# Split passes in the outer stages of a long convolution, and its spectrum loaded once

## The chip, the cores and the metric

The kernel runs on one core of a Trainium2 chip. The metric is the device time of one execution in microseconds (us). It took 3428.81 us in the median of 3 runs (3427.15 to 3435.29).

The core's engines work side by side, each through its own instructions in a fixed order: TensorE (PE, with PEld for its weight loads), VectorE (DVE), ScalarE (ACT), GpSimd (POOL) and SyncE (SP), whose queue issues nearly all DMA transfers here. An instruction that waits holds up all that stand behind it on its engine.

## The reference

One layer of an encoder, sequence 2048, width 1024, fp32. A projection feeds two groups of heads: a Hyena group (512 channels) and an mLSTM group (512 channels). Their outputs are normalised, projected, added; cross-attention and a squared-ReLU MLP follow. What matters here is the Hyena group:

```python
def _hyena(hy, spec, skip):
    L = hy.shape[1]
    u = hy.astype(jnp.float32)
    z, g1, g2 = u[..., :D_HYENA], u[..., D_HYENA:2 * D_HYENA], u[..., 2 * D_HYENA:]
    for o, gate in enumerate((g1, g2)):
        conv = jnp.fft.irfft(jnp.fft.rfft(z, n=2 * L, axis=1) * spec[:, o], n=2 * L, axis=1)[:, :L]
        z = gate * (conv + z * skip[o].astype(jnp.float32))
    return z
```

So there are two rounds, each a real FFT of length 4096, a product with the spectrum of a filter, an inverse FFT, and a gate. The second round's result is normalised in groups of 64 channels.

## The kernel before, in words

`program` (L1615) puts the phases in order, and `weave` (L1597) mixes two of them as Python generators: each yields a cost after a piece of work, and the one that is behind in its share goes on. `filters` (L158) makes the spectra of both rounds and writes them to DRAM (`hd`), mixed with the first projection passes. `hyena` (L628) is mixed with the rest of the input projection (`sweep` L502, `natural` L595). Then come `mlstm` (L761) mixed with the last projection pieces and `memproj`, and `attention` mixed with the rest of mLSTM, and the MLP. The program is not run in the written order: `schedule_with_timeline_sim` (L1584) lets a scheduler reorder each engine's instructions before the build, so the diff alone does not give the order on an engine.

`hyena` writes each FFT as two small DFTs with data in DRAM between them. The sequence is laid out as 128 partitions x 16 columns `j`, each of 512 channels. One round `o` has three stages:

- Stage 1 (L700 to L713), 8 steps of two columns. `load1` brings `z` (512 KB); each column is multiplied by the two parts of `f1` (L710, fp32, 128x512), ScalarE and VectorE in turn copy the results out of PSUM (`copy`, L137), and two stores write them to `zs`.
- Stage 2 (L715 to L732), 16 steps of two frequency blocks. `load2` (L655) brings the step's matrices `dm` and `em`, the data `t` (512 KB), and the spectrum: `hr` gets the real part and `hi` the imaginary part, each 64 rows, loaded twice so that both partition halves hold them (L664 to L666, four transfers of 256 KB). For each of two blocks: a matmul by `dm` (L724), two ScalarE copies that exchange the halves (L726, L727), a VectorE product with `hr` (L728), a GpSimd product with `hi` (L729), a VectorE sum (L730), and, one block later (`late`), the matmul back by `em` (L692) with its ScalarE evacuation (L693). When both are out, a store to `zg` (L695). The loads of step i+1 are asked for at the start of step i.
- Stage 3 (L734 to L759), 8 steps of two columns. `load3` brings two parts of `zg` and the gate; for each column two accumulated matmuls by the parts of `e2` (L743) and a VectorE product with the gate (L744). In the first round the result goes to `z1`, the second round's input. In the second it is squared on GpSimd (L751), summed and normalised on VectorE (L753 to L756, with `rsqrt` L144), multiplied by a gain on GpSimd (L758) and stored.

All these tiles come from two rings: tag `a` (128 x 2 x 512, 10 buffers) and tag `b` (128 x 512, 5 buffers); PSUM gives the convolution four banks (`hy`, L124) and the projection four others (`mm`, L121). mLSTM's first tiles take the memory that the convolution leaves, so it begins when `hyena` is through.

The projection does not use fp32 matmuls. It splits each operand into a high part, rounded to fp32r by a ScalarE cast, and a low part, the rest, by a VectorE subtraction (`split`, L299), and adds three passes:

```python
    def mm3(self, ps, lh, ll, rh, rl, start, stop):
        mm = self.nc.tensor.matmul
        mm(ps, lh, rh, start=start, stop=False)
        mm(ps, lh, rl, start=False, stop=False)
        mm(ps, ll, rh, start=False, stop=stop)
```

The functions that the diff touches, and what calls them:

Of the kernel before, what the change touches and what calls it, by code (L numbers as in the profile page):

```python
# [9 lines left out]
F32 = mybir.dt.float32  # L10
F32R = mybir.dt.float32r
I32 = mybir.dt.int32
AF = mybir.ActivationFunctionType
ALU = mybir.AluOpType
# [6 lines left out]
CH = 512  # L21
# [76 lines left out]
class Prog:  # L98
# [22 lines left out]
    def mm(self):  # L121
        return self.ps.tile([128, 512], F32, tag="mm", name="mm", bufs=4)
# [170 lines left out]
    def mm3(self, ps, lh, ll, rh, rl, start, stop):  # L293
        mm = self.nc.tensor.matmul
        mm(ps, lh, rh, start=start, stop=False)  # L295
        mm(ps, lh, rl, start=False, stop=False)  # L296
        mm(ps, ll, rh, start=False, stop=stop)  # L297

    def split(self, hi, lo, src):  # L299
        self.nc.scalar.copy(hi, src)  # L300
        self.nc.vector.tensor_tensor(lo, src, hi.bitcast(F32), ALU.subtract)  # L301
# [326 lines left out]
    def hyena(self, es):  # L628
        nc, tc, a = self.nc, self.tc, self.a
        hy = self.dram("hy", (3, L, CH)).rearrange("s (q j) c -> s q j c", j=16)  # L630
        hd = self.dram("hd", (2, 32, 128, CH))
        yh = self.dram("yh", (L, CH)).rearrange("(q j) c -> q j c", j=16)
        z1 = self.dram("z1", (128, 16, CH))
        sds = [self.dram(f"zs{o}", (2, 128, 16, CH)) for o in range(2)]
        gds = [self.dram(f"zg{o}", (2, 128, 16, CH)) for o in range(2)]
        sb = es.enter_context(tc.tile_pool(name="h_sb", bufs=1, side="right"))

        def ta():
            return sb.tile([128, 2, CH], F32, tag="a", name="a", bufs=10)

        def tb():
            return sb.tile([128, CH], F32, tag="b", name="b", bufs=5)

        f1 = sb.tile([128, 2, 128], F32, name="f1")
        e2 = sb.tile([128, 2, 128], F32, name="e2")
        nc.sync.dma_start(out=f1, in_=a["c_f1"])
        nc.sync.dma_start(out=e2, in_=a["c_e2"])
        ghy = self.bcast(sb, a["hy_norm_g"], CH, "ghy")
        def load1(o, j2):
            z = ta()  # L650
            js = slice(2 * j2, 2 * j2 + 2)
            nc.sync.dma_start(out=z, in_=hy[0, :, js] if o == 0 else z1[:, js])
            return z

        def load2(o, i):  # L655
            p, k = divmod(2 * i, 16)
            dm = sb.tile([128, 2, 128], F32, tag="dm", name="dm", bufs=2)
            em = sb.tile([128, 2, 128], F32, tag="em", name="em", bufs=2)
            nc.sync.dma_start(out=dm, in_=a["c_dm"][:, 2 * i:2 * i + 2])
            nc.sync.dma_start(out=em, in_=a["c_em"][:, 2 * i:2 * i + 2])  # L660
            t, hr, hi = ta(), ta(), ta()
            nc.sync.dma_start(out=t, in_=sds[o][p, 8 * k:8 * k + 16].rearrange("(k r) j c -> (r j) k c", k=2))
            src = hd[o, 2 * i:2 * i + 2].rearrange("k (r l) c -> r l k c", r=2)
            for h in range(2):  # L664
                nc.sync.dma_start(out=hr[64 * h:64 * h + 64], in_=src[0])
                nc.sync.dma_start(out=hi[64 * h:64 * h + 64], in_=src[1])  # L666
            if i == 0:
                nc.sync.dma_start(out=hr[64:65, 0], in_=hd[o, 0, 64:65])
                nc.vector.memset(hi[0:1, 0], 0.0)
                nc.vector.memset(hi[64:65, 0], 0.0)  # L670
            return dm, em, t, hr, hi

        def load3(o, j2):
            js = slice(2 * j2, 2 * j2 + 2)
            r = [ta() for p in range(2)]
            for p in range(2):
                nc.sync.dma_start(out=r[p], in_=gds[o][p, :, js])
            gate = ta()
            nc.sync.dma_start(out=gate, in_=hy[1 + o, :, js])
            return r, gate  # L680

        held = []

        def late(f):
            if held:
                held.pop()()
            if f is not None:
                held.append(f)

        def back(m, em, y, gs, dst):  # L690
            pg = self.hy()
            nc.tensor.matmul(pg, em[:, m], y, start=True, stop=True)  # L692
            nc.scalar.copy(gs[:, m], pg)  # L693
            if m == 1:
                nc.sync.dma_start(out=dst.rearrange("(k r) j c -> (r j) k c", k=2), in_=gs)  # L695

        for o in range(2):
            sd, gd = sds[o], gds[o]
            q = [load1(o, 0), load1(o, 1)]
            for j2 in range(8):  # L700
                yield 3.5
                js = slice(2 * j2, 2 * j2 + 2)
                z = q.pop(0)
                if j2 < 6:
                    q.append(load1(o, j2 + 2))
                st = [ta() for p in range(2)]
                for jj in range(2):
                    for p in range(2):
                        pp = self.hy()
                        nc.tensor.matmul(pp, f1[:, p], z[:, jj], start=True, stop=True)  # L710
                        self.copy(st[p][:, jj], pp)
                for p in range(2):
                    nc.sync.dma_start(out=sd[p, :, js], in_=st[p])  # L713
            nxt = load2(o, 0)
            for i in range(16):  # L715
                yield 3.5
                p, k = divmod(2 * i, 16)
                dm, em, t, hr, hi = nxt
                if i < 15:
                    nxt = load2(o, i + 1)  # L720
                gs = ta()
                for m in range(2):
                    pp = self.hy()
                    nc.tensor.matmul(pp, dm[:, m], t[:, m], start=True, stop=True)  # L724
                    xt, y = tb(), tb()
                    nc.scalar.activation(xt[0:64], pp[64:128], AF.Copy, scale=-1.0)  # L726
                    nc.scalar.copy(xt[64:128], pp[0:64])  # L727
                    nc.vector.tensor_tensor(y, pp, hr[:, m], ALU.mult)  # L728
                    nc.gpsimd.tensor_tensor(xt, xt, hi[:, m], ALU.mult)  # L729
                    nc.vector.tensor_tensor(y, y, xt, ALU.add)  # L730
                    late(lambda m=m, em=em, y=y, gs=gs, dst=gd[p, 8 * k:8 * k + 16]: back(m, em, y, gs, dst))
            late(None)  # L732
            nxt = load3(o, 0)
            for j2 in range(8):  # L734
                yield 3.5
                js = slice(2 * j2, 2 * j2 + 2)
                r, gate = nxt
                if j2 < 7:
                    nxt = load3(o, j2 + 1)
                for jj in range(2):  # L740
                    pp = self.hy()
                    for p in range(2):
                        nc.tensor.matmul(pp, e2[:, p], r[p][:, jj], start=p == 0, stop=p == 1)  # L743
                    nc.vector.tensor_tensor(gate[:, jj], pp, gate[:, jj], ALU.mult)  # L744
                if o == 0:
                    nc.sync.dma_start(out=z1[:, js], in_=gate)
                    continue
                y = gate.rearrange("q j (g e) -> q (j g) e", g=8)
                sq = ta()
                sqv = sq.rearrange("q j (g e) -> q (j g) e", g=8)  # L750
                nc.gpsimd.tensor_tensor(sqv, y, y, ALU.mult)  # L751
                ms = sb.tile([128, 16], F32, tag="ms", name="ms", bufs=2)
                nc.vector.tensor_reduce(ms, sqv, AX.X, ALU.add)  # L753
                nc.vector.tensor_scalar(ms, ms, 1.0 / 64, EPS, ALU.mult, ALU.add)
                rv = self.rsqrt(sb, ms, "hr")
                nc.vector.tensor_tensor(sqv, y, rv.unsqueeze(2).broadcast_to([128, 16, 64]), ALU.mult)  # L756
                for jj in range(2):
                    nc.gpsimd.tensor_tensor(sq[:, jj], sq[:, jj], ghy, ALU.mult)  # L758
                nc.sync.dma_start(out=yh[:, js], in_=sq)  # L759
# [919 lines left out]
```

## Time and profile before

The profiled execution took 3428.81 us, its span from the first to the last instruction is 3427.1 us, and the mean granted TensorE clock is 0.971 of full speed.

| part of the span | from, to (us) |
|---|---|
| filters with the first projection passes | to about 470 |
| round one: stage 1, 2, 3 (first to last matmul) | 474.5 to 527, 534.6 to 714, 717.6 to 777 |
| round two: stage 1, 2, 3 | 777.6 to 843, 854.5 to 1059, 1064.1 to 1128 |
| mLSTM's first VectorE work | 1153.9 |
| attention and MLP, to the end | from about 1430 |

How to read the lines that follow: a window row gives, for one stretch, the busy time of PE, PEld, DVE, ACT and POOL with the number of instructions, then the granted clock, the mean busy share of the 16 DMA engines and GB/s. A group row gives line, engine, operation, tiles written and read, shapes and count, then the sum of busy time in us and the mean of one in ns, then the idle time ahead of it with what ended most of it. A timeline row gives start (us), duration (us), engine, line and operation, and in brackets the idle time ahead of it and what ended it. Matmuls are pipelined: the duration of one overlaps the next, so their cost is read from start to start.

### The profile page before, as it was taken

How to read it: one execution, taken by the hardware profiler on the slowest of the kernel's cores; microseconds unless marked ns; L12 is line 12 of the kernel's file. 1: busy time of each engine (PE TensorE's matmuls, PEld its weight loads, DVE VectorE, ACT ScalarE, POOL GpSimd, SP SyncE). 2: the span in 40 equal slices, each digit the busy share in tenths (PEclk: the TensorE clock that was granted, in tenths of full speed). 3: DMA queues.
4: the chain of work that ended last, by engine and by line, in shares of the span. 5: the costliest groups of instructions: out<-in, count | busy, mean ns of one | idle time of the engine just before them, and what ended most of it. 6: DMA issues, size and time to landing. Idle time of an engine off the chain costs nothing.

```text
span 3427.1 us, 46184 instructions
## 1 busy us (share of the span) xinstructions
PE 3213.8 (94%) x15671; PEld 2573.1 (75%) x15671; DVE 2129.9 (62%) x3855; ACT 1246.8 (36%) x2403; POOL 1265.2 (37%) x878
## 2 busy tenths in 40 slices
PE   6999999899999978699999998999899999999997
PEld 5656666677666978588888897788788887888876
DVE  7585225434547657766755343888986785555695
ACT  4344435623553333333333333322322243333335
POOL 2131001200223222333324012888776667444483
PEclk9999999999999989899999999999999999999998
DMA  5366889996899499867758546665654465444434
GB/s 163 114 207 203 285 282 251 285 338 229 234 252 286 137 287 294 254 215 253 248 206 283 194 166 223 207 202 194 190 172 151 157 234 174 118 148 136 132 96 157
DMA packets 477129, 715.93 MB, mean 209 GB/s; under 512 B 41195, under 2 KB 259377, under 8 KB 467677
## 3 DMA queue, kind: packets, MB, share of 16 engines
q1 hardware_dynamic: 475288, 710.11, 65.0%
q0 software_dynamic: 1600, 2.86, 0.4%
q8 instruction: 124, 2.03, 0.3%
q14 instruction: 113, 0.92, 0.1%
q10 hardware_dynamic: 4, 0.00, 0.0%
HBM read 485.26 MB, written 227.57 MB: 208 GB/s over the span
## 4 chain that ended last, share of the span: by engine, by line
PE 43%; DMA 7%; DVE 6%; POOL 4%; issue 3%; ACT 1%; SPq 0%; DVEq 0%; POOLq 0%; ACTq 0%
PE mm L297 9%; PE mm L295 9%; PE mm L296 9%; PE hy L297 4%; PE hy L295 4%; PE hy L296 4%; POOL acc L1477 1%; DVE al L1277 1%; DVE rw L947 1%; PE hy L1103 1%; PE hy L895 1%; DMA wn<-in_w_out_dram 1%; DMA vw<-o 1%; PE hy L974 1%; DMA kn<-kn 1%
## 5 line engine op out<-in xcount | busy, mean ns | idle before, releaser
L1276 ACT CAST ah<-w 128x512 fp32r<-128x512 f32 x286 | 175.2, 622 | 514.3 <-PE hy L296 185.6
L1277 DVE TENSOR_TENSOR bl<-wr,bh 128x512 fp32r<-128x512 f32 x213 | 238.5, 1127 | 148.0 <-ACT bh L1276 146.8
L295 PE MATMUL mm<-xh,wh 128*128 128x512 f32 (+1 forms) x768 | 316.6, 413 | 11.5 <-ACT P L532 5.5
L296 PE MATMUL mm<-xl,wh 128*128 128x512 f32 (+1 forms) x768 | 303.0, 395 | 0.3 <-DVE xr_y L150 0.2
L297 PE MATMUL mm<-xh,wl 128*128 128x512 f32 (+1 forms) x768 | 302.7, 394 | 0.3 <-DVE wl L301 0.3
L729 POOL TENSOR_TENSOR b<-b,a 128x512 f32<-128x512 f32 x64 | 89.0, 1392 | 497.6 <-DVE a L670 224.4
L1277 DVE TENSOR_TENSOR al<-w,ah 128x512 fp32r<-128x512 f32 x234 | 230.1, 985 | 54.3 <-ACT ah L1276 54.3
L301 DVE TENSOR_TENSOR wl<-wn,wh 128x512 fp32r<-128x512 f32 (+1 forms) x224 | 163.6, 758 | 120.7 <-ACT wh L300 120.1
L297 PE MATMUL mm<-bh,al 128*128 128x512 f32 x576 | 222.9, 394 | 11.3 <-POOL al L1277 8.9
L1276 ACT CAST bh<-wr 128x512 fp32r<-128x512 f32 x232 | 143.5, 621 | 238.6 <-PE mm L297 181.2
L295 PE MATMUL mm<-bh,ah 128*128 128x512 f32 x576 | 226.4, 393 | 0.1
L296 PE MATMUL mm<-bl,ah 128*128 128x512 f32 x576 | 225.3, 391 | 0.0
L295 PE MATMUL mm<-act,wh 128*128 128x512 f32 x512 | 203.7, 401 | 6.3 <-DMA wh<-vw 4.5
L297 PE MATMUL mm<-act,wl 128*128 128x512 f32 x512 | 203.5, 401 | 4.6 <-DMA wl<-vw 4.6
L296 PE MATMUL mm<-act,wh 128*128 128x512 f32 x512 | 204.6, 400 | 0.0
L300 ACT CAST wh<-wn 128x512 fp32r<-128x512 f32 (+1 forms) x224 | 130.4, 619 | 197.9 <-PE mm L296 76.5
L295 PEld LDWEIGHTS mm<-xh,wh 128*128 128x128 f32 x768 | 148.4, 193 | 60.4 <-issue 18.4
L1142 POOL TENSOR_TENSOR ssum<-ssum,sq 128x512 f32<-128x512 f32 x56 | 75.0, 1340 | 310.9 <-ACT sq L1141 310.6
L296 PEld LDWEIGHTS mm<-xl,wh 128*128 128x128 f32 x768 | 147.8, 192 | 45.8 <-issue 19.9
L297 PEld LDWEIGHTS mm<-xh,wl 128*128 128x128 f32 x768 | 147.6, 192 | 42.2 <-issue 15.8
L295 PE MATMUL hy<-bh,ah 128*128 128x512 f32 x448 | 175.4, 392 | 1.7 <-DVE acc L1553 1.7
L296 PE MATMUL hy<-bl,ah 128*128 128x512 f32 x448 | 174.7, 390 | 0.0
(371 smaller groups left out, 8991.3 us busy)
## 6 DMA issues: line engine op xcount, KB each, us to landing
wr<-hc SPq DMA_DIRECT2D x224, 256.0 KB
w<-in_ff_w_dram SPq DMA_DIRECT2D x176, 256.0 KB
a<-hd SPq DMA_DIRECT2D x128, 256.0 KB
hc<-t SPq DMA_DIRECT2D x128, 256.0 KB
wn<-in_w_in_dram SPq DMA_DIRECT2D x104, 256.0 KB
hc<-q SPq DMA_DIRECT2D x96, 256.0 KB
fs<-a SPq DMA_DIRECT2D x32, 512.0 KB
a<-fs SPq DMA_DIRECT2D x32, 512.0 KB
```

The costliest lines, as they stand in the source:

```text
L295: mm(ps, lh, rh, start=start, stop=False)
L296: mm(ps, lh, rl, start=False, stop=False)
L297: mm(ps, ll, rh, start=False, stop=stop)
L300: self.nc.scalar.copy(hi, src)
L301: self.nc.vector.tensor_tensor(lo, src, hi.bitcast(F32), ALU.subtract)
L729: nc.gpsimd.tensor_tensor(xt, xt, hi[:, m], ALU.mult)
L895: nc.tensor.matmul(pc[:, 129 * i:129 * i + 129], kk[:, 2 * p + i], ve[:, 2 * p + i], start=True, stop=True)
L947: nc.vector.scalar_tensor_tensor(nm[:, h], nm[:, h], GC[:, r + h:r + h + 1], masks[d], ALU.add, ALU.min)
L974: nc.tensor.matmul(dst, nm[:, h], va[:, h], start=True, stop=state is None)
L1142: nc.gpsimd.tensor_tensor(ssum, ssum, sq, ALU.add)
L1276: self.nc.scalar.copy(hi, src)
L1277: eng.tensor_tensor(lo, src, hi.bitcast(F32), ALU.subtract)
```

## The change

In stages 1 and 3 of both rounds the fp32 matmuls by `f1` and `e2` become three split passes (`mm3`). The constants are split once at the start of `hyena`; the moving data is split by the new `halved`: a ScalarE cast and a subtraction, on VectorE for `z` and for the first part of stage 3, on GpSimd for the second. In `load2` the real spectrum is loaded into the lower half of `hr` alone and the imaginary one into the upper half of `hi` alone; two ScalarE copies fill the other halves. Tag `a` has 9 buffers instead of 10, tag `b` 7 instead of 5.

```diff
+    def halved(self, pool, src, eng, **kw):
+        hi, lo = (pool.tile(list(src.shape), F32R, **(kw or {"name": n})) for n in ("ch", "cl"))
+        self.nc.scalar.copy(hi, src)
+        eng.tensor_tensor(lo, src, hi.bitcast(F32), ALU.subtract)
+        return hi, lo
...
-            return sb.tile([128, 2, CH], F32, tag="a", name="a", bufs=10)
+            return sb.tile([128, 2, CH], F32, tag="a", name="a", bufs=9)
...
-            return sb.tile([128, CH], F32, tag="b", name="b", bufs=5)
-
-        f1 = sb.tile([128, 2, 128], F32, name="f1")
-        e2 = sb.tile([128, 2, 128], F32, name="e2")
-        nc.sync.dma_start(out=f1, in_=a["c_f1"])
-        nc.sync.dma_start(out=e2, in_=a["c_e2"])
+            return sb.tile([128, CH], F32, tag="b", name="b", bufs=7)
+
+        consts = []
+        for n in ("c_f1", "c_e2"):
+            t = ta()[:, 0, 0:256].rearrange("p (a b) -> p a b", a=2)
+            nc.sync.dma_start(out=t, in_=a[n])
+            h, l = (sb.tile([128, 2, 128], F32R, name=n + x) for x in "hl")
+            nc.scalar.copy(h, t)
+            nc.vector.tensor_tensor(l, t, h.bitcast(F32), ALU.subtract)
+            consts.append((h, l))
+        f1, e2 = consts
...
-            for h in range(2):
-                nc.sync.dma_start(out=hr[64 * h:64 * h + 64], in_=src[0])
-                nc.sync.dma_start(out=hi[64 * h:64 * h + 64], in_=src[1])
+            nc.sync.dma_start(out=hr[0:64], in_=src[0])
+            nc.sync.dma_start(out=hi[64:128], in_=src[1])
+            nc.scalar.copy(hr[64:128], hr[0:64])
+            nc.scalar.copy(hi[0:64], hi[64:128])
...
                 for jj in range(2):
+                    zh, zl = self.halved(sb, z[:, jj], nc.vector, tag="b", name="b", bufs=7)
                     for p in range(2):
                         pp = self.hy()
-                        nc.tensor.matmul(pp, f1[:, p], z[:, jj], start=True, stop=True)
+                        self.mm3(pp, f1[0][:, p], f1[1][:, p], zh, zl, True, True)
...
                     for p in range(2):
-                        nc.tensor.matmul(pp, e2[:, p], r[p][:, jj], start=p == 0, stop=p == 1)
+                        rh, rl = self.halved(sb, r[p][:, jj], (nc.vector, nc.gpsimd)[p], tag="b", name="b", bufs=7)
+                        self.mm3(pp, e2[0][:, p], e2[1][:, p], rh, rl, p == 0, p == 1)
```

## The prediction

> **What bounds the kernel now.** First the page: one core, TensorE busy nearly all the time, the other engines far from it.
>
> ```profile
> span 3427.1 us, 46184 instructions
> PE 3213.8 (94%) x15671; PEld 2573.1 (75%) x15671; DVE 2129.9 (62%) x3855; ACT 1246.8 (36%) x2403; POOL 1265.2 (37%) x878
> ```
>
> An average over stages says little, so next I cut the two convolution rounds into windows at the first and last matmuls of L710 (stage 1), L724 and L692 (stage 2) and L743 (stage 3). The last two columns are the DMA share and GB/s, the one ahead of them the granted clock.
>
> ```profile
> core 0: us, PE busy (x) PEld busy (x) DVE busy (x) ACT busy (x) POOL busy (x), PEclk, DMA share, GB/s
> 474.00:530.00 56.00, 55.48 (x204) 35.62 (x205) 22.49 (x34) 18.96 (x31) 0.00 (x0) 1.00 0.76 264
> 530.00:712.00 182.00, 167.05 (x700) 118.46 (x698) 92.80 (x161) 102.81 (x168) 43.21 (x32) 0.98 1.01 274
> 712.00:772.00 60.00, 60.00 (x351) 45.88 (x350) 15.53 (x25) 9.71 (x22) 0.00 (x0) 1.00 0.97 367
> 772.00:846.00 74.00, 72.16 (x416) 54.05 (x415) 27.34 (x65) 26.11 (x57) 0.00 (x0) 1.00 0.62 218
> 846.00:1062.00 216.00, 200.81 (x779) 140.18 (x778) 114.98 (x202) 112.49 (x186) 45.77 (x32) 0.97 0.92 245
> 1062.00:1130.00 68.00, 65.40 (x324) 48.07 (x323) 59.26 (x143) 17.88 (x33) 28.59 (x18) 0.97 0.86 292
> 1160.00:1430.00 270.00, 206.77 (x1448) 193.56 (x1447) 184.25 (x497) 95.47 (x215) 62.69 (x49) 0.86 0.83 255
> ```
>
> Read three things. Stages 1 and 3 of the first round and stage 1 of the second are TensorE's: 55.5 of 56, 60 of 60, 72 of 74 us busy. Stage 2 is where TensorE stands still (15 us in each round), and in the first round the DMA engines are full there (1.01). Stage 3 of the second round is VectorE's: 59 of 68 us. The last row is the stretch behind the convolution, in which TensorE idles 63 of 270 us: work taken off TensorE is not worth its whole time there.
>
> **The change part by part.**
>
> *Three passes for one fp32 matmul.* An fp32 matmul shows as two records (L710 x2), a split one as three (L295, L296, L297). Durations overlap, so I take start to next start.
>
> ```profile
> 488.67 1.02 PE L710 MATMUL hy<-a,f 128*128 128x512 f32 x2
> 489.53 0.27 PE L566 MATMUL mm<-ident,cv 128*63 128x128 f32 x1
> ```
> ```profile
> 479.87 0.39 PE L295 MATMUL mm<-xh,wh 128*128 128x512 f32 x1
> 480.10 0.39 PE L296 MATMUL mm<-xl,wh 128*128 128x512 f32 x1
> 480.33 0.39 PE L297 MATMUL mm<-xh,wl 128*128 128x512 f32 x1
> 480.56 0.39 PE L295 MATMUL mm<-xh,wh 128*128 128x512 f32 x1
> ```
>
> fp32: 489.53 - 488.67 = 0.86 us. Split: 480.56 - 479.87 = 0.69 us. There are 2 rounds x 2 stages x 32 = 128 such matmuls: 128 x 0.17 = **-22 us** of TensorE, where the window rows show it full, or at the head of VectorE's tail.
>
> *The casts and subtractions.* Stage 1 gets 16 casts on ScalarE and 16 subtractions on VectorE in each round, stage 3 gets 32 casts, 16 subtractions on VectorE and 16 on GpSimd. The nearest rows of the same shape:
>
> ```profile
> L300 ACT CAST wh<-wn 128x512 fp32r<-128x512 f32 x60 | 34.2, 618 | 58.7 <-DMA wn<-in_w_in_dram 43.5 <-PE mm L296 9.8 <-PE mm L297 5.3
> L301 DVE TENSOR_TENSOR wl<-wn,wh 128x512 fp32r<-128x512 f32 x60 | 42.0, 728 | 49.9 <-ACT wh L300 49.8
> L1277 POOL TENSOR_TENSOR al<-w,ah 128x512 fp32r<-128x512 f32 x52 | 73.9, 1424 | 120.0 <-ACT ah L1276 120.0
> L546 ACT ACTIVATE cv<-P,cb,cw 128x1008 f32<-128x1008 f32 x10 | 12.3, 1232 | 0.2
> ```
>
> ScalarE gains 96 x 0.62 = 59 us, VectorE 64 x 0.73 = 47, GpSimd 32 x 1.42 = 46. In stages 1 and in stage 3 of the first round these engines are busy at most 45% and TensorE's own work hides them; without that cover they would cost their own time. But ScalarE now waits for the loads that TensorE waited for, and the evacuations of the projection stand behind it: the cast row shows that it already waits 43.5 us for weight loads. I take **+4 us** (0 to 12, the latter one 0.4 us in each of 32 steps).
>
> *The spectrum.* Two of four loads of 256 KB go per step, 64 in all, or 16.8 MB; two copies of 64 partitions x 1024 come, 1.24 us each by the L546 row: 64 x 1.24 = 79 us more for ScalarE. In stage 2 of the first round that makes 102.8 + 39.7 = 142.5 of 182 us. Nothing is lost by the sum; the question is what the copies wait for. At present a step takes (704.4 - 534.6) / 15.5 = 10.95 us in round one, (1050.4 - 854.5) / 15.5 = 12.6 in round two:
>
> ```profile
> L724 PE MATMUL hy<-a,dm x64: 590/592/667, 534.6 to 704.4; 128*128 128x512 f32 x64
> L724 PE MATMUL hy<-a,dm x64: 590/592/1061, 854.5 to 1050.4; 128*128 128x512 f32 x64
> ```
>
> In the built order of the changed kernel, the copies of step i+1 stand on ScalarE behind the first half of step i and directly ahead of the second evacuation of step i-1. The loads of step i+1 stand on the SP queue behind the store of step i-2, which waits for that step's second evacuation. So from one such evacuation to the next the path runs through a whole transfer: store, three issues, flight, two copies, evacuation. Before, only GpSimd and VectorE waited for these loads, a step later:
>
> ```profile
> 549.20 0.39 SPq L662 DMA_DIRECT2D a<-zs  x1
> 549.63 0.58 SPq L665 DMA_DIRECT2D a<-hd  x1
> 550.26 0.61 SPq L666 DMA_DIRECT2D a<-hd  x1
> 573.10 0.57 SPq L665 DMA_DIRECT2D a<-hd  x1
> 582.65 0.69 DVE L728 TENSOR_TENSOR b<-hy,a 128x512 f32<-128x512 f32 x1 [5.63 <-DMA a<-hd]
> 530.22 0.88 SPq L666 DMA_DIRECT2D a<-hd  x1
> 537.64 0.48 DVE L669 MEMSET a<- 1x512 f32 x1 [7.59 <-DMA a<-hd]
> L693 ACT COPY a<-hy 128x512 f32<-128x512 f32 x64 | 37.4, 584 | 49.1 <-PE hy L692 47.8 <-DMA kn<-st 0.9
> ```
>
> From the issue of t to that of hi pass 550.26 - 549.20 = 1.06 us, with the store ahead of it (as long as t, 0.4, and a gap) 1.55. A flight took 582.65 - 573.10 = 9.55 us in the full stage and 537.64 - 530.22 = 7.42 at its start. I take 8.3, nearer the middle, since a sixth of the stage's traffic goes. The copies: the first partly runs before the second has landed, so 1.24 plus 0.1; the evacuation 0.58. Sum 1.55 + 8.3 + 1.34 + 0.58 = 11.8 us a step against 10.95: 16 x 0.85 = **+14 us** in round one. Bounds: if the path is hidden, TensorE's own need decides, and the 182 us window holds 15 us of stillness, of which 11 can go: -11. If the flight stays 9.55 and a weight load is queued ahead (0.6 and its wait): 13.9, or +47. In round two the changed order gives TensorE more projection work per step, some 13.0 us, so the same path is just covered: **+3 us** (-10 to +14). What stands behind the waiting copy is the evacuation of the back matmul and that of the projection, and TensorE waits for both when their buffers are used up.
>
> One buffer less of tag a, two more of tag b, and constants split at the start: the loads still run one step ahead, the rest is four casts and subtractions, under 3 us beside other work; nothing.
>
> *The tail.* Stage 3 of round two ends on VectorE, not on TensorE: its last matmul starts at 1128.2, the last normalising multiply at 1147.1, and mLSTM begins only after that.
>
> ```profile
> L743 PE MATMUL hy<-a,e x64: 590/592/595, 1064.1 to 1128.2; 128*128 128x512 f32 x64
> L756 DVE TENSOR_TENSOR a<-a,hr_y x8: 1214/1224/1228, 1090.5 to 1147.1; 128x1024 f32<-128x1024 f32 x8
> 1127.98 1.89 POOL L751 TENSOR_TENSOR a<-a 128x1024 f32<-128x1024 f32 x1 [2.44 <-DVE hr_y L155]
> 1128.02 1.89 DVE L153 TENSOR_TENSOR hr_t<-hr_y 128x16 f32<-128x16 f32 x1
> 1129.94 0.17 DVE L154 SCALAR_TENSOR_TENSOR hr_t<-hr_t,ms 128x16 f32<-128x16 f32 x1
> ```
>
> To that come 16 subtractions on VectorE, 16 x 0.73 = 11.7 us. GpSimd gets 16 of 1.42 there, and the rows show what a GpSimd operation does to a small VectorE one beside it: 1.89 us instead of 0.17. If half of the 16 catch one for 1.0 us, that is 8 more. **+20 us** (9, if the lock-step is hidden and part of the work fits gaps; 27, if nearly every one catches). The Trainium skill, SBUF — State Buffer, Who interferes with whom, says that a VectorE instruction with two inputs in SBUF and a GpSimd one that reads SBUF exclude each other for the whole instruction. The 1.89 us row agrees; by the rule the subtractions would block as well, 16 x 1.4 = 23 instead of 8, an estimate, and the sum would be 15 us higher.
>
> *Credit.* The built order moves about 12 us of projection passes (counted at 0.23 us) ahead of mLSTM's first matmul. That work is missing behind it, where TensorE idles a quarter of the time: half of it counts, **-6 us** (-12 to 0).
>
> Sum: -22 + 14 + 3 + 4 + 20 - 6 = +13 us. The profiled execution took 3428.81 us, of which its span is 3427.1; it is itself the median of the three runs shown, so the sum is made on 3428.8: **3442 us**. About 0.3% (10 us) is what a measurement of this kernel can tell from no change.
>
> **The rivals.**
>
> *The cover holds.* ScalarE's waits vanish because the flight falls with the traffic. For it: DMA is at 1.01 and 16.8 MB go. Against it: flights of 7.4 us at the stage's start. With a flight under 6.8 us a step is under 10.3 and TensorE decides: -22 - 9 - 4 + 2 + 15 - 6 = -24, **3405 us**, faster. It decides from a flight of about 7.3 us downward.
>
> *Stage 2 stays as it is* (flight 7.5 us), and passes and tail cancel: -22 + 0 + 0 + 4 + 20 - 6 = -4, **3425 us**.
>
> *The gate is worse.* Flights of 9.5 us with weight loads queued between: +47 in round one, +14 in round two, the rest as forecast: 13 + 33 + 11 = +57, **3486 us**. For it: in the built order such loads stand between store and spectrum in about every third step. Against it: traffic falls.
>
> *Four passes.* The split saves a whole pass, 0.23 us, on each matmul: 128 x 0.23 = 30 instead of 22, so 3434 us. Against it: the two fp32 records take 0.86 us, not 4 x 0.23 = 0.92. The Trainium skill, FP8 and Floating Point Precision, TensorE Precision Notes, states four passes for true FP32; the rows come close and are what the sum uses.
>
> That the passes don't come: the built order has 384 split passes where 128 fp32 matmuls stood, so this is no case.
>
> **How the numbers follow.** The gate on ScalarE and the tail together (forecast, 3442): 0.43. The worse gate (3486): 0.05. Both are slower: 0.48. The cover holds (3405): 0.32, faster. Stage 2 as it is (3425) 0.15 and four passes (3434) 0.05: within 0.3%, 0.20. The range is 3400 to 3482: it takes in the faster rival and the forecast with its flight at 9.55 us, and leaves out the far ends of the bounds. The forecast's own range is 3432 to 3475.
>
> **What would show it.** Right: copies on ScalarE whose wait is for DMA a<-hd, tens of us in sum; a step of stage 2 in round one near 11.8 us; the two passes at 0.69 us; the last L756 multiply 15 to 25 us later behind the first matmul of its stage than now (83 us). Wrong: a step under 10.5 us with no ScalarE wait for loads; a tail as long as now; or a stretch from mLSTM's start to attention that shrinks or grows by more than 10 us, which I have only as a credit.

## The result, and the profile after

The changed kernel takes 3437.99 us (median of 11 runs, 3432.14 to 3441.1), the kernel before 3429.64 beside it (median of 11, 3422.11 to 3435.7). The ratio is 1.0024, with a 95% interval of 1.0015 to 1.0034: 8.4 us more by the medians, slower, but by less than the 0.3% that was set as the bound for a difference. The forecast was 3442, thirteen more than the profiled execution of before. The profiled execution of the changed kernel took 3436.39 us. Its page begins:

```profile
span 3434.7 us, 46699 instructions
PE 3197.1 (93%) x15799; PEld 2595.0 (76%) x15799; DVE 2190.4 (64%) x3921; ACT 1360.7 (40%) x2563; POOL 1313.3 (38%) x910
```

TensorE works 16.7 us less than before (3213.8) and the span is 7.6 us longer. So TensorE stands still for 24.3 us more, and the question is where. The windows of the changed kernel follow, cut as those of before at the first and last matmuls of the stages: stage 1, 2, 3, then 1 and 2 of round two; the tail up to mLSTM's first VectorE work; mLSTM up to attention's first transpose. (The last rows of the view, its sum, are left out.)

```profile
474.00:531.00 57.00, 55.40 (x264) 45.70 (x264) 34.38 (x56) 29.33 (x51) 0.00 (x0) 1.00 0.83 280
531.00:716.00 185.00, 168.73 (x684) 117.44 (x685) 94.41 (x160) 134.46 (x199) 47.04 (x32) 0.96 0.76 219
716.00:778.00 62.00, 62.00 (x434) 57.78 (x433) 30.39 (x42) 29.56 (x58) 22.35 (x16) 1.00 0.93 354
778.00:838.00 60.00, 56.70 (x379) 51.18 (x378) 34.15 (x77) 31.98 (x68) 0.00 (x0) 1.00 0.77 271
838.00:1060.00 222.00, 206.62 (x802) 144.90 (x802) 113.75 (x205) 147.08 (x223) 43.63 (x32) 0.96 0.70 197
1060.00:1179.00 119.00, 103.98 (x697) 95.65 (x696) 102.77 (x200) 43.50 (x85) 62.49 (x41) 0.96 0.65 216
1179.00:1441.00 262.00, 189.09 (x1328) 175.33 (x1327) 187.34 (x504) 86.42 (x202) 63.84 (x54) 0.86 0.83 256
```

The two stretches of before that the prediction did not show whole, the tail up to mLSTM and mLSTM up to attention:

```profile
1062.00:1154.00 92.00, 89.40 (x526) 72.07 (x525) 76.97 (x182) 20.82 (x41) 39.07 (x25) 0.98 0.76 253
1154.00:1427.00 273.00, 210.38 (x1488) 197.64 (x1487) 186.27 (x508) 96.60 (x218) 64.12 (x54) 0.87 0.83 254
```

Length of a row less its PE column is TensorE's stillness. In stage 2 it hardly moved: 16.3 us against 14.9 in round one, 15.4 against 15.2 in round two, although the DMA share there fell from 1.01 to 0.76 and from 0.92 to 0.70. In the tail it is 15.0 against 2.6, and in mLSTM 72.9 against 62.6. The other stages of the convolution have 2.5 us more (1.1, 0 and 1.4). So most of the change's loss stands in the tail and behind it, and stage 2, with a sixth of its traffic gone, gained nothing. The experiments ask why.

The waits of all engines in stage 2 of round one of the changed kernel (us in total, times, longest):

```profile
POOL b L742 <- ACT b L740: 192.3, 30, 70.5
ACT a L677 <- DMA a<-hd: 39.1, 12, 5.0
DVE b L741 <- ACT b L740: 38.3, 14, 6.8
...
PE hy L704 <- DVE b L743: 10.2, 5, 3.1
DVE b L743 <- POOL b L742: 9.9, 16, 0.7
```

The first row is mostly time in which GpSimd has nothing to do: it is busy for 47 of the 185 us, and one wait of 70.5 us reaches back before the stage. Read on from the second row: ScalarE's first copy (L677) waits 39 us for the spectrum; VectorE's product (L741) waits as long for ScalarE's exchange of the halves (L740), which stands behind that copy; the sum (L743) waits for the product on GpSimd; and TensorE's matmul back (L704) waits for the sum. Over both rounds the first link is 83.2 us in 27 waits; in the kernel before ScalarE waits for these loads not once.

### The profile page after: what moved, and what is told of

Read it like the earlier page. It is cut to its first block, busy times and chain, and to the rows that moved or that the text cites. A ratio compares the mean times of both kernels' runs of the same rounds, so it can differ in the third digit from the quotient of the medians.

```text
span 3434.7 us, 46699 instructions
## 1 busy us (share of the span) xinstructions
PE 3197.1 (93%) x15799; PEld 2595.0 (76%) x15799; DVE 2190.4 (64%) x3921; ACT 1360.7 (40%) x2563; POOL 1313.3 (38%) x910
## 4 chain that ended last, share of the span: by engine, by line
PE 70%; DVE 10%; DMA 9%; issue 6%; ACT 2%; POOL 2%; SPq 1%; DVEq 0%; ACTq 0%; POOLq 0%
PE mm L297 15%; PE mm L295 15%; PE mm L296 14%; PE hy L297 5%; PE hy L296 5%; PE hy L295 5%; PE hy L284 2%; DMA a<-hd 1%; PE mm L572 1%; PE hy L238 1%; DVE bl L1291 1%; PE hy L1117 1%; PE hy L253 1%; DMA rw<-rows 1%; DVE rw L961 1%
## 5 line engine op out<-in xcount | busy, mean ns | idle before, releaser
L297 PE MATMUL mm<-bh,al 128*128 128x512 f32 x576 | 223.3, 395 | 11.7 <-POOL al L1291 8.9
L307 DVE TENSOR_TENSOR wl<-wn,wh 128x512 fp32r<-128x512 f32 (+1 forms) x224 | 160.9, 744 | 91.7 <-ACT wh L306 90.8
```

## The experiments

The kernels ran in three groups, each on a chip with its own runs of the kernel before, whose median lay between 3424.8 and 3431.1 us. Compare them by the ratio to before, not by the microseconds; 0.001 is 3.4 us. The ratio is the one on record; the quotient of the two medians differs from it by up to 0.0017 (e8). "Stillness" is TensorE's idle time in stage 2 of round one / round two, in one profiled execution each, from windows cut at each kernel's own stages. The five kernels with four loads have 11.9 to 20.2 us of it in round one, and e1 and e4, which differ only in the last stage of round two, 20.2 and 14.4; so a difference of less than some 6 us tells nothing by itself.

| kernel | spectrum in stage 2 | last stage, round two | stillness (us) | ratio to before (95%) |
|---|---|---|---|---|
| before | four loads | fp32 | 14.9 / 15.2 | 1 |
| changed | copies on ScalarE | split | 16.3 / 15.4 | 1.0024 (1.0015 to 1.0034) |
| e1 | four loads | split | 20.2 / 17.0 | 1.0014 (0.9999 to 1.0028) |
| e2, no passes at all | copies on ScalarE | fp32 | 20.4 / 16.5 | 1.0036 (1.0024 to 1.0047) |
| e3 | copies on ScalarE | fp32 | 16.4 / 13.0 | 1.0022 (1.0008 to 1.0036) |
| e4 | four loads | fp32 | 14.4 / 17.4 | 0.9993 (0.9978 to 1.0008) |
| e5, before with nine buffers a | four loads | fp32 | 17.8 / 15.4 | 0.9988 (0.9973 to 1.0002) |
| e6, e4 with ten buffers a | four loads | fp32 | 11.9 / 17.4 | 0.9974 (0.9962 to 0.9986) |
| e7 | copies on GpSimd | split | 5.2 / 6.7 | 0.9968 (0.9956 to 0.9980) |
| e8 | copies on ScalarE | split, no GpSimd | 18.2 / 15.1 | 1.0039 (1.0020 to 1.0058) |
| e9 | copies on ScalarE, no wait for the load | split | 3.6 / 13.4 | 0.9965 (0.9952 to 0.9979) |
| e10 | copies on VectorE | split | 6.3 / 8.3 | 0.9969 (0.9958 to 0.9981) |
| e11 | copies on GpSimd | fp32 | 2.2 / 1.8 | 0.9947 (0.9934 to 0.9961) |
| e12, no passes at all | copies on GpSimd | fp32 | 6.0 / 7.9 | 0.9980 (0.9967 to 0.9992) |

### One part at a time: e1 to e4

e1, passes without the copies:

```diff
-            nc.sync.dma_start(out=hr[0:64], in_=src[0])
-            nc.sync.dma_start(out=hi[64:128], in_=src[1])
-            nc.scalar.copy(hr[64:128], hr[0:64])
-            nc.scalar.copy(hi[0:64], hi[64:128])
+            for h in range(2):
+                nc.sync.dma_start(out=hr[64 * h:64 * h + 64], in_=src[0])
+                nc.sync.dma_start(out=hi[64 * h:64 * h + 64], in_=src[1])
```

> The changed kernel with the spectrum loaded four times again, as before; split passes and buffer numbers as changed. Theory (the ScalarE copies gate stage 2): ScalarE's 83 us of waits for DMA a<-hd are gone, a step of stage 2 in round one falls from 11.45 to about 10.9 us, the tail of round two (first matmul by e2 to last normalising multiply) stays at 105 to 115 us, and the time falls by 5 to 12 us, to some 3426 to 3433. Rival one (the halved traffic was a gain, the loss lies elsewhere): DMA share in stage 2 back at 1.0, the step stays at 11.4 or grows, time 3438 to 3446. Rival two (9 instead of 10 buffers slowed stage 2): the step stays at 11.4 and the time within 3 us of 3438.

Measured: ScalarE's waits for the spectrum fall to 2.0 us, but the step of stage 2 in round one stays at 11.54 us (changed: 11.45), and the time hardly falls, to a ratio of 1.0014. A miss for the theory: with the heavy traffic back, the stage stands still for another reason. A step longer by itself was also a poor witness. The build puts different amounts of projection work into a stage each time, so from here on stillness is compared, not the step.

e2, copies without the passes: the kernel before with the four lines of `load2` that the diff adds.

> The kernel before with only the spectrum edit: two loads and two ScalarE copies; fp32 matmuls, 10 and 5 buffers. Theory: ScalarE waits 60 to 100 us for DMA a<-hd, the step in round one goes from 10.95 to about 11.5 us and the one in round two from 12.6 to about 13, the tail stays at about 83 us, time 3436 to 3446. Rival one (16.8 MB less traffic is a gain): step 10.5 us, time 3415 to 3425. Rival two (nothing of it matters): 3427 to 3432.

Measured: 3440.56 us, ratio 1.0036, some 12 us slower than before, with 79.8 us of ScalarE waiting for the spectrum in 25 waits, steps of 11.5 and 13.1 us, and 20.4 / 16.5 us of stillness. That is the theory, but for the tail, which took 88 us. The copies edit loses by itself.

e3, the changed kernel with the last stage of round two in fp32:

```diff
                     for p in range(2):
+                        if o == 1:
+                            nc.tensor.matmul(pp, ef[:, p], r[p][:, jj], start=p == 0, stop=p == 1)
+                            continue
                         rh, rl = self.halved(sb, r[p][:, jj], (nc.vector, nc.gpsimd)[p], tag="b", name="b", bufs=7)
```

> The changed kernel, but stage 3 of round two keeps its fp32 matmuls (no casts and subtractions there); all else as changed. Theory (the tail on VectorE and GpSimd delays mLSTM): the tail falls from 112 to about 83 us, mLSTM's first VectorE work comes at 1150 to 1157 instead of 1179 us, and the time falls by 8 to 18 us, to some 3420 to 3430. Rival (the tail's delay is made good behind it anyway, because projection work has been pulled ahead): mLSTM begins 25 us earlier but the time stays within 4 us of 3438.

e4, the same with the four loads of e1:

> Both together: split passes in stage 1 of both rounds and stage 3 of round one only, spectrum loaded four times. Theory: neither gate nor longer tail, three quarters of the 22 us of passes remain: 3412 to 3422, faster than both kernels. Rival one (gate theory wrong): as the one with the tail alone. Rival two (passes are worth nothing here, since TensorE idles behind the convolution): 3427 to 3432.

Measured: in e3 mLSTM begins at 1157.6 us instead of 1179.3, but attention at 1436.4 instead of 1441.2, and the time is a ratio of 1.0022: 22 us earlier at one place, under 1 us at the end by the ratios. So the theory missed and the rival had it. In e4 the ratio falls to 0.9993, and its 3426.03 us miss the theory's 3412 to 3422. e3's windows of the tail and of mLSTM:

```profile
1060.00:1158.00 98.00, 89.65 (x527) 71.08 (x527) 82.01 (x183) 25.02 (x48) 37.37 (x25) 0.97 0.70 241
1158.00:1436.00 278.00, 209.52 (x1471) 195.32 (x1469) 181.97 (x507) 94.90 (x213) 65.77 (x54) 0.87 0.81 248
```

Set them beside the same two rows of the changed kernel. The longer tail there holds 104.0 us of TensorE work where e3 has 89.7, and mLSTM then needs 189.1 where e3 needs 209.5. A long tail is not empty: projection passes run in it that otherwise fill mLSTM. So a delay of mLSTM's start is given back in part by attention's start: 17 of 22 us between e3 and the changed kernel, 11 of 22 between e4 and e1.

### Buffers, engines, the tail: e5 to e8

e5 is the kernel before with one buffer of tag `a` less:

```diff
-            return sb.tile([128, 2, CH], F32, tag="a", name="a", bufs=10)
+            return sb.tile([128, 2, CH], F32, tag="a", name="a", bufs=9)
```

> The kernel before with nine instead of ten buffers of tag a and nothing else. In the run with split passes and four loads, and in the one with the last stage left in fp32, the step of stage 2 stayed at 11.4 to 11.5 us although ScalarE no longer waited for loads. Theory A: the ring of nine buffers does that (loads of t and of the spectrum wait for a buffer). Then the step of stage 2 in round one rises here from 10.95 to 11.3 or more, TensorE stands still there for 19 us or more instead of 14.9, and the time is 3433 to 3438 us. Theory B: the ring has slack, and the step is longer because the faster stage 1 leaves other projection work for stage 2. Then the step stays at 10.9 to 11.1, and the time at 3427 to 3433.

e6 is e4 with ten buffers of tag `a` and five of tag `b`:

> Split passes in stage 1 of both rounds and in stage 3 of round one, the last stage of round two in fp32, four loads of the spectrum, and ten buffers of tag a, five of tag b: the passes without either of the two losses, and with the ring of before. Theory A (the ring of nine costs): step of stage 2 near 10.95, 3419 to 3423 us, clearly below before. Theory B (it doesn't): step 11.3 to 11.5 as with nine, 3424 to 3428, about the time of the same kernel with nine buffers (3426). Rival to both: the saving on TensorE, 96 matmuls x 0.17 = 16 us, is real but is lost again at mLSTM's start, so that nothing under 3427 can be had.

Measured: with nine buffers the step rises to 11.3 us, as theory A had it; with ten, in e6, it is back at 10.93. The ring of nine thus explains most of the step of e1: the three kernels with four loads and nine buffers have 11.30 to 11.54 us (e4 11.35), the two with ten 10.93 and 10.95. The stillness doesn't follow as plainly (17.8 in e5, a little under A's 19, but 14.4 in e4). And e5's time isn't longer than that of before, where A wanted 2 to 7 us more. That the ring costs time isn't shown: e6 lies in A's range with 3420.72 us, and at 0.9974 beside e4's 0.9993 it points that way, but their intervals overlap.

e7 moves the copies to GpSimd:

```diff
-            nc.scalar.copy(hr[64:128], hr[0:64])
-            nc.scalar.copy(hi[0:64], hi[64:128])
+            nc.gpsimd.tensor_copy(hr[64:128], hr[0:64])
+            nc.gpsimd.tensor_copy(hi[0:64], hi[64:128])
```

> The changed kernel with the two copies across partition halves on GpSimd instead of ScalarE: GpSimd is the engine that waits for these loads anyway, and only the product with hi stands behind them. Theory (the wait on ScalarE, ahead of its evacuations, is what the copies cost): ScalarE's 83 us of waiting for a<-hd go to about 0, GpSimd waits for them instead, TensorE stands still in stage 2 no more than with four loads, and the time is 3432 to 3437 us, a little under the changed kernel's 3438. Rival: copies on GpSimd are longer (two of some 2 us, or more beside VectorE) and a whole step's product stands behind them, so that the step of stage 2 passes 12 us and the time 3442.

Measured: 3418.32 us, ratio 0.9968, better than the theory's best: 19 us less than the changed kernel by the ratios. GpSimd's own line in e7's waits, and the windows of stage 2 in both rounds:

```profile
POOL a L677 <- DMA a<-hd: 188.8, 24, 67.7
```

```profile
531.00:725.00 194.00, 188.76 (x909) 142.83 (x910) 106.70 (x168) 109.44 (x183) 82.61 (x64) 0.99 0.75 220
838.00:1050.00 212.00, 205.26 (x836) 147.54 (x835) 119.60 (x166) 120.49 (x188) 81.21 (x65) 0.98 0.72 209
```

Two of GpSimd's 24 waits, 67.7 and 54.7 us, stand ahead of its first copy in each round, where it has nothing else to do; the other 22 make 66 us, not much less than ScalarE's 83, and TensorE stands still for only 5.2 and 6.7 us. But the first row also has 909 matmul records in 194 us where the changed kernel has 684 in 185. The scheduler, with the copy elsewhere, put half as many projection passes again into this stage. More cover or no wait: e7 alone can't tell, and e9 and e10 were made for that.

e8 takes GpSimd out of the tail's subtractions:

```diff
-                        rh, rl = self.halved(sb, r[p][:, jj], (nc.vector, nc.gpsimd)[p], tag="b", name="b", bufs=7)
+                        rh, rl = self.halved(sb, r[p][:, jj], (nc.vector, nc.gpsimd if o == 0 else nc.vector)[p], tag="b", name="b", bufs=7)
```

> The changed kernel with all 32 subtractions of the last stage of round two on VectorE, none on GpSimd. Theory (VectorE's own work is the tail; what is added to it is the subtractions, 16 more x 0.73 to 0.9 = 12 to 14 us, less what GpSimd no longer blocks): the last normalising multiply falls 105 to 120 us behind the first matmul of the stage, against 112 now, and because the delay is filled with projection passes the time moves by no more than 4 us, 3434 to 3442. Rival (the GpSimd subtractions block VectorE for their whole length, 24 us): the tail falls under 100 us and the time to 3432 or less.

Measured: the last normalising multiply starts at 1164.8 us, 7.7 earlier than in the changed kernel, some 107 behind the stage's beginning; the time is 3438.63 us, a ratio of 1.0039, no less than the changed kernel's. Both lie in the theory's ranges. The tail of e8 up to mLSTM's first VectorE work:

```profile
1058.00:1171.70 113.70, 102.71 (x718) 95.22 (x716) 101.65 (x217) 45.20 (x88) 42.09 (x25) 0.98 0.69 226
```

VectorE has 16 subtractions more than in the changed kernel and is busy for no longer (101.65 us against 102.77), and the tail is 5 us shorter. So GpSimd's subtractions did hold VectorE up, but not for their whole length, which would have brought the tail under 100 us.

### The wait or the order: e9 to e12

e9 keeps the copies on ScalarE, but they read a constant tile, so that half of each spectrum tile is left out of the computation:

```diff
-            nc.scalar.copy(hr[64:128], hr[0:64])
-            nc.scalar.copy(hi[0:64], hi[64:128])
+            nc.scalar.copy(hr[64:128], spare[0:64].unsqueeze(1).broadcast_to([64, 2, CH]))
+            nc.scalar.copy(hi[0:64], spare[64:128].unsqueeze(1).broadcast_to([64, 2, CH]))
```

> The changed kernel, whose two ScalarE copies read a constant tile instead of the half just loaded; the copied halves of the spectrum are therefore left out (zeros). ScalarE's work and the DMA traffic are those of the changed kernel, and the built order has about as many projection passes in a step of stage 2 as its own (some 33); only the wait for the load is gone from ScalarE. With the copies on GpSimd TensorE stood still for 5 and 7 us in the two stages 2 instead of 16 and 15, but that build also had half as many projection passes again in the first of them, so that the wait and the order were not told apart. Theory A (the wait on ScalarE): stillness of 5 to 9 us in each stage 2 and 3418 to 3427 us. Theory B (the order, that is how many passes cover a step): 14 to 17 us of stillness as in the changed kernel, and 3433 to 3440.

e10 has them on VectorE (`nc.vector.tensor_copy` in the place of `nc.scalar.copy`):

> The changed kernel with the two copies on VectorE: projection passes are placed nearly as in the changed kernel (some 33 in a step). Theory A (what counts is that the wait doesn't stand ahead of the evacuations on ScalarE): ScalarE's wait for a<-hd goes, TensorE's stillness in stage 2 falls under 10 us a round, 3420 to 3428 us. Theory A2 (the wait costs on any engine with much work behind it; VectorE has two products, a sum and evacuations of the projection behind it): stillness 12 to 18 us, 3432 to 3440. Theory B (the order): the same as A2, so only a fall speaks for A against both.

Stage 2 of both rounds in e9, and then in e10:

```profile
531.00:698.50 167.50, 163.90 (x720) 118.16 (x719) 93.27 (x163) 133.43 (x199) 41.10 (x32) 1.00 0.80 236
816.00:1040.00 224.00, 210.59 (x862) 151.30 (x860) 121.44 (x220) 158.13 (x241) 45.86 (x33) 0.99 0.71 209
```

```profile
530.00:698.00 168.00, 161.66 (x660) 114.20 (x660) 118.74 (x190) 101.29 (x165) 46.12 (x32) 0.97 0.80 236
826.00:1042.00 216.00, 207.72 (x810) 146.00 (x811) 143.36 (x238) 117.78 (x193) 46.10 (x33) 0.97 0.72 212
```

Round one settles it. In e9 ScalarE is as busy as in the changed kernel (133.4 us against 134.5) and the number of matmuls is near its own (720 against 684), and the stillness is 3.6 us instead of 16.3. In e10 there are fewer matmuls than in the changed kernel (660), and the stillness is 6.3. TensorE's work in the stage is less in both (163.9 and 161.7 us, 168.7 in the changed kernel), so it isn't more cover. The ratios, 0.9965 and 0.9969, put the two at some 3418 and 3419 beside a kernel before of 3430 us, at the lower edge of theory A's ranges. The waits of e10 in that window suggest why the same wait is harmless on VectorE (GpSimd's row, the first, is left out):

```profile
ACT a L705 <- PE hy L704: 21.2, 12, 4.6
DVE a L677 <- DMA a<-hd: 20.1, 10, 6.7
...
DVE b L741 <- ACT b L740: 12.1, 8, 4.0
```

VectorE waits 20.1 us for the spectrum, but the product that follows needs the spectrum anyway; the evacuations and exchanges of ScalarE go on, and now ScalarE waits for TensorE (21.2 us; 4.2 in the changed kernel). No line of the matmul back waiting for VectorE's sum is among the long ones any more: 1.3 us instead of 10.2. A2 and B are out for round one. In round two e9 still stands still for 13.4 us, with no wait for the spectrum; e10, e7 and e12 have 6.7 to 8.3 there. But 11.0 of e9's 13.4 us lie in the first 50 us of its window. Behind these it has 2.4 us, e10 0.3, and the changed kernel 8.8: there too the stillness goes with ScalarE's wait. What holds up the head of that stage stays open.

e11 is e7 with the fp32 tail of e3, e12 the kernel before with e7's copies and no passes:

> Copies on GpSimd and the last stage of round two left in fp32: both losses taken out of the change, its gains kept. If the tail's extra length costs what it cost beside four loads (3436.8 against 3426.0), 3406 to 3413 us. If it costs what it cost beside copies on ScalarE (3438 against 3436), 3415 to 3419. Tail from the first e2 matmul to the last normalising multiply about 85 us instead of 107.

> The kernel before with two loads of the spectrum and the two copies on GpSimd, and nothing else (no split passes, ten and five buffers). Theory A: the lighter traffic without a wait on ScalarE is the whole gain: TensorE's stillness in each stage 2 falls from 15 to 5 to 8 us, 3412 to 3420 us. Rival: the gain of the copies on GpSimd needs the passes' time as well, and 3424 to 3431 is measured.

Measured: e11 takes 3404.61 us beside 3424.81 for before, 0.9947 (0.9934 to 0.9961), the fastest kernel of the study, 18 us under before; e12 0.9980 (0.9967 to 0.9992), 7 us under before. e11 is at 3412 by its ratio and 3430, where the tail's extra length costs what it cost beside four loads; its tail took 90 us, not 85. e12 has the stillness of its theory A; its 3416.85 us lie in A's range, its ratio (3423) just above it. Lighter traffic without a wait on ScalarE, in the order that the scheduler makes of it, thus gives 7 us; splitting 96 matmuls without the tail another 11; and splitting the tail as well (e7) loses 7 of those again.

Two pairs give the price of the place of the copies, with the order that comes with it: e2 against e12, without passes, 1.0036 against 0.9980; the changed kernel against e7, 1.0024 against 0.9968. Both are 0.0056, or 19 us.

## Why the prediction was right or wrong, by its steps

The sum came out 4 us from the result, and 13 us were forecast where 8.4 came. Its sign and its mechanism were right, its steps less so than their sum. One chain of edits leads from before over e4 and e3 to the changed kernel. The split matmuls without the tail, forecast at three quarters of -22 and +4, or -12.5 us, came to -2 (-9 with ten buffers, e6); the copies, forecast at 17, to 10; the split tail, forecast at 20 - 6 less a quarter of 22, or 8.5, to 1. Each is uncertain by some 6 us. In this chain the gain and both losses came out smaller than forecast, and that the total came so near is in part luck.

**Three passes for one fp32 matmul: confirmed.** The changed kernel in stage 1 of round one:

```profile
492.87 0.39 PE L295 MATMUL hy<-b,c_f1h 128*128 128x512 f32 x1
493.10 0.40 PE L296 MATMUL hy<-b,c_f1h 128*128 128x512 f32 x1
493.33 0.39 PE L297 MATMUL hy<-b,c_f1l 128*128 128x512 f32 x1
493.56 0.40 PE L295 MATMUL hy<-b,c_f1h 128*128 128x512 f32 x1
```

493.56 - 492.87 = 0.69 us, as forecast. TensorE's work fell by 16.7 us in this pair, but between kernels with the same matmuls it varies by some 10: 3209.1 to 3221.3 us in the four without passes, 3190.1 to 3198.8 in the six with all 128 split. By the means the split saves 19 us, near the forecast's 22, and the rival of four passes, which wanted 30, is not borne out. The Trainium skill, FP8 and Floating Point Precision, TensorE Precision Notes, counts four passes through the array for true FP32. The rows don't speak against the count: four in 0.86 us would be 0.215 us each, an estimate, where a split pass takes 0.23; what failed is to price them by the split pass. At the end, e11 against e12 (96 matmuls, 16 us by the same rate) gives 11 us, and e6 against before 9, each uncertain by some 6: too wide to tell 16 from the 12 that are left with the casts.

**Casts and subtractions in stages 1 and 3: not contradicted.** +4 us was forecast, and the stillness of the three windows rose by 2.5; no run has them by themselves.

**The spectrum's gate on ScalarE: right in mechanism, mis-sized by what it was set against.** This is the path as the changed kernel ran it, first on ScalarE and then on the SP queue:

```profile
609.66 1.05 ACT L678 COPY a<-a 64x1024 f32<-64x1024 f32 x1
610.61 0.57 ACT L705 COPY a<-hy 128x512 f32<-128x512 f32 x1
...
619.80 1.05 ACT L677 COPY a<-a 64x1024 f32<-64x1024 f32 x1 [3.84 <-DMA a<-hd]
620.87 1.05 ACT L557 ACTIVATE cv<-cv 128x1008 f32<-128x1008 f32 x1
621.94 1.04 ACT L678 COPY a<-a 64x1024 f32<-64x1024 f32 x1
622.89 0.57 ACT L705 COPY a<-hy 128x512 f32<-128x512 f32 x1
```

```profile
600.75 0.38 SPq L707 DMA_DIRECT2D zg<-a  x1
...
611.21 0.36 SPq L707 DMA_DIRECT2D zg<-a  x1
611.67 0.42 SPq L670 DMA_DIRECT2D dm<-in_c_dm_dram  x1
612.19 0.79 SPq L673 DMA_DIRECT2D a<-zs  x1
613.02 0.58 SPq L675 DMA_DIRECT2D a<-hd  x1
...
623.49 0.38 SPq L707 DMA_DIRECT2D zg<-a  x1
```

Follow it: the evacuation at 610.61, the store at 611.21, the loads of `dm`, `t` and of the spectrum behind it, the spectrum there at 619.80, the two copies with a step of the projection between them, the next evacuation at 622.89 and its store at 623.49. From store to store that is 10.46 us (600.75 to 611.21) and 12.28 (to 623.49); the mean over the stage is (708.6 - 531.1) / 15.5 = 11.45, against 11.8 forecast and 10.95 before. Two sizes inside are off. The flight is 6.8 us (613.02 to 619.80; 5.5 to 7.4 in eleven of the stage's twelve waits), not 8.3, and other work stands in the path that was not counted: the load of `dm`, 0.5, and a projection operation between the copies, 1.05. That is also why the rival "the cover holds" failed although its condition came true: it was to decide from a flight of 7.3 us downward, and the flight is 6.8.

What the sum lacked is the other side. The step of before was taken as what the stage would stay at without a gate; but e12 and e10 show that with a sixth of the traffic gone, and in their orders, TensorE stands still only 6 to 8 us per round, instead of 15. The gate took that back, 9.9 and 7.1 us of stillness (changed kernel less e10), and so the net in stage 2 is +1.5 us instead of +17. In stage 2 by itself the rival "stage 2 stays as it is" was nearest, for a reason that it didn't name: not that nothing happened, but that a gain and a loss of the same size met. At the end the copies edit costs 12 us against the kernel before (e2), 10 between e4 and e3, and 3 between e1 and the changed kernel: all under the term.

**The tail: right in cause, and nearly in size.** From the first matmul by `e2` to the last normalising multiply it took 83 us, and takes 112 (1060.5 to 1172.5): +29, where +20 was forecast. Not all of that is the split's: with the rest of the kernel alike, the split tail is longer by 22 us (e3, 90), 21 (e4 to e1, 84 to 106) and 24 (e11 to e7, 90 to 114). Some of the VectorE groups that grew, in the tail of the changed kernel and then of before (busy us, mean ns of one):

```profile
L302 DVE TENSOR_TENSOR b<-a,b 128x512 fp32r<-128x512 f32 x15 | 13.5, 903 | 0.0
L770 DVE TENSOR_TENSOR a<-a,hr_y 128x1024 f32<-128x1024 f32 x8 | 12.6, 1569 | 0.1
L307 DVE TENSOR_TENSOR wl<-wn,wh 128x512 fp32r<-128x512 f32 x12 | 9.6, 824 | 1.2 <-ACT wh L306 1.2
L154 DVE SCALAR_TENSOR_TENSOR hr_t<-hr_t,ms 128x16 f32<-128x16 f32 x24 | 8.8, 372 | 0.2
```

```profile
L756 DVE TENSOR_TENSOR a<-a,hr_y 128x1024 f32<-128x1024 f32 x8 | 9.8, 1222 | 0.1
L301 DVE TENSOR_TENSOR wl<-wn,wh 128x512 fp32r<-128x512 f32 x8 | 5.8, 730 | 1.2 <-ACT wh L300 1.2
L154 DVE SCALAR_TENSOR_TENSOR hr_t<-hr_t,ms 128x16 f32<-128x16 f32 x24 | 5.7, 242 | 0.3
```

The subtractions themselves take 13.5 us (forecast 11.7). Single groups say little of what GpSimd's subtractions hold up: e8, which has none of them, has 450 ns for L154 and 1110 for L307. VectorE's whole work in the window rows says more. It is 102.8 us against 77.0 before; 15 new subtractions and four more of the projection (L307), at 0.73 us, make 13.9, and 12 are lengthening. Against e3 (82.0) the lengthening is 7. In e8, 31 and four subtractions at 0.73 make 25.6 of the 24.7 us that it has more than before, so nothing is left. GpSimd's 24.1 us of subtractions thus lengthened VectorE's work by some 7 to 12 us, where the forecast had 8. The Trainium skill's rule (SBUF — State Buffer, Who interferes with whom) would have made 23 of it, by the estimate in the prediction. The trace reaches half of that at most. The longer stage also takes in work of the projection: the four subtractions and, on TensorE, 104.0 us of work instead of 89.4.

**The credit: the step that failed.** The prediction moved 12 us of projection passes ahead of mLSTM and counted half, -6; it named as a sign of error that the stretch from mLSTM's start to attention changes by over 10 us. It does: from 272.9 us (1153.9 to 1426.8) to 261.9 (1179.3 to 1441.2). The work in the projection's PSUM tiles (`mm`) alone, in the tail and in that stretch of the changed kernel and then of before:

```profile
1060.00:1179.00 119.00, 84.41 (x601) 81.47 (x600) 2.90 (x11) 10.44 (x27) 0.96 0.65 216
1179.00:1441.00 262.00, 147.42 (x959) 128.05 (x958) 46.24 (x125) 37.63 (x69) 0.86 0.83 256
```

```profile
1062.00:1154.00 92.00, 69.82 (x462) 61.32 (x461) 2.88 (x11) 7.96 (x20) 0.98 0.76 253
1154.00:1427.00 273.00, 166.07 (x1118) 146.44 (x1116) 46.41 (x125) 40.28 (x77) 0.87 0.83 254
```

mLSTM's stretch lost 18.7 us of it (166.07 to 147.42), not 12, and gave back 11.0 us, or 59%, not half. So of 25.4 us of delay at mLSTM's start 14.4 are left at attention's. The split tail's price at the end, from three pairs: 1.0024 against 1.0022 (e3), 1.0014 against 0.9993 (e4), 0.9968 against 0.9947 (e11), or 1, 7 and 7 us, each uncertain by some 6. The terms of the prediction for that stage were 20 - 6 and a quarter of the 22 saved: 8.5.

Together, in the two profiled executions: 16.7 us of TensorE's work less; stillness +2.5 in stages 1 and 3, +1.5 in stage 2, +22.7 in the tail and mLSTM, and -2.4 elsewhere: 24.3 - 16.7 = 7.6 us, the difference of the spans. The last comes from stretches the change doesn't touch (+2.1 ahead of 474 us, -6.5 in attention, +1.9 behind it) and is left as the spread of single executions: e3 and e8 have the same work there and attention windows of 689 and 690 us, as before has, against 681 in the changed kernel.

## What to carry to other kernels

A wait for a transfer belongs on an engine whose next work needs that transfer anyway. Ahead of the evacuations on ScalarE, the same two copies cost 19 us more here than on GpSimd or VectorE, which waited for the same data; and with those two the time was, within the intervals, that of e9, which doesn't wait at all. When an edit both lightens a queue and adds a wait, price the two against a stage with neither, since a stage that looks unchanged may hide a gain and a loss of equal size; and count a saving or a delay at the engine's end of the next stage, not at its own, where other work flows in to fill it.

## What the runs showed of the hardware

- A load of 256 KB took 9.55 us from issue to use in the full stage of before, with the DMA share at 1.01, and 6.8 in the changed kernel with the share at 0.76. Part of that is its place: before, it was issued behind 1 MB of its own step, after behind 512 KB.
- A copy of 64 partitions x 1024 fp32 between partition halves took 1.05 us on ScalarE, 1.04 in the median on GpSimd (e7; 1.17 to 1.23 as the mean in stage 2 of round one) and 0.69 in the median on VectorE (e10). These differences are small beside what the place of the wait costs.
- One buffer less in a ring of ten lengthened the step of stage 2 in round one from 10.95 to 11.3 us, without a longer time for the kernel (0.9988, 0.9973 to 1.0002).
